# Reordering the planned front of a hybrid encoder layer: S5 output quarters among the attention projections, first scores behind the gated linear unit, row and output-matrix tiles in halves

## The chip, the cores and the metric

One Trainium2 chip, one of its cores, one launch per run. The metric is device time in microseconds (us); a figure quoted as "the time" is the median of three runs.

## The reference

One encoder layer on 1024 tokens of width 1024. The input projection feeds three mixers, whose concatenated outputs go through one output matrix; a mixture of 16 experts follows.

```python
x = layer_norm(x, ln_in_g, ln_in_b)
proj = h @ w_in                    # q,k,v,g of retention | u of S5 | q,k,v of attention
ret  = retention(q, k, v, g, theta)            # 8 chunks of 128 tokens, 4 heads
y    = gelu(S5 states -> outputs + d * u)      # 16 groups of 16 channels
s5   = y * sigmoid(y @ w_glu + b_glu)          # the gated linear unit
att  = window_sink_attention(q, k, v, sink)    # 8 heads, 128-key window, blocks of 128 queries
h    = LN(alpha*h + concat(ret, s5, att) @ w_out)
h    = LN(alpha*h + ExpertChoiceSwiGLU(h))     # 16 experts, width 2048
```

## The kernel before

Every fp32 product of a projection is made of three matmuls on a high and a low half (`mm3`, L74 to L76); `split` writes the high half on ScalarE (ACT, L65 or L125) and the low half on VectorE (DVE, L66).

The work up to the attention scores is `front()`. It is a list of places: `at(place, fn)` gives a step a number, and the steps are then issued in the order of those numbers, so each engine's order is written out by hand. Its parts, in the order of the program:

- The input rows are normed (`Norm`: load `x`, L147 statistics, L152 the power `l0rs` on GpSimd (POOL), L155 and L158 on DVE), turned, and split into the row tiles `hT` (high and low, all 1024 tokens each). Beside that a chain of small operations on POOL (`rsmall`, L254 to L262) works out the retention decays, and ACT takes their exponentials (`w` L266, `dec` L268). The rows of keys and values of chunk 0 follow (`ktok` L193).
- A string `order` then names products: `K`, `V` and `g` (keys, values, gates), `r0` to `r7` (retention outputs), `q00` to `q31` (attention query quarters, 24 matmuls each, whose results go through `kst` and `q_d` stores), and `o0` to `o3`, the S5 output quarters (`Output.product`, L798 and L801, from the tiles `MU`, `W`, `Z`, and `Output.put`, a Gelu on ACT into `YG`, L805). Before, the `o` quarters stand last.
- Behind `o3` the gated linear unit (GLU): four `turn` (transposes of `YG`, L813, then `yT` on ACT, L814), four `gate` (L819) and four `gated` (L827).
- `Matrix` loads the output matrix in four pieces of 1 MB (L901) and splits each into `WO` (ACT L65, DVE L66). `hT` and `WO` take turns in the same two buffers of the pool `hy`: no piece of `WO` can be written until the last product has read `hT`.

Behind `front()` the order on each engine is set by a scheduler that simulates the program. There `attention_keys` loads the keys `KHL` (four 512 KB transfers, L1250) and values `AV` (two, L1252), and `attention_scores(i)` loads `qs` (L1275), all three issued by POOL; it multiplies scores (L1283, L1284), takes the maximum on DVE (L1286) and the exponential on ACT (L1291, L1293). `attention_out(i)` scales (L1307), turns (`pT`, L1313) and multiplies with `AV` (`po`). The output projection multiplies `yh`, `yl` with `WO`. The expert stage is again in a hand-written order and streams 402 MB of weights.

Of the kernel before, what the change touches and what calls it, by code (L numbers as in the profile page):

```python
# [15 lines left out]
OP = mybir.AluOpType  # L16
# [114 lines left out]


class Norm:

# [34 lines left out]
    def parts(self, q):  # L169
        K = self.K  # L170
        ts = slice(self.t * P, (self.t + 1) * P)
        split(K, K.hT[0][:, q * 4:q * 4 + 4, ts], K.hT[1][:, q * 4:q * 4 + 4, ts], self.pt.pop(q))


class Project:
# [5 lines left out]
    def part(self, c0, c1):  # L181
        K, ts = self.K, slice(self.t * P, (self.t + 1) * P)
        if c0 == 0:
            self.ps = K.pmm.tile([P, 512], F32, name="mm")
        for c in range(c0, c1):
            w = self.W[c // 4].u[c // 2 % 2]
            b = [x.rearrange("p (c f) -> p c f", c=2)[:, c % 2, :] for x in w]
            mm3(K.nc, self.ps, [K.hT[s][:, c, ts] for s in range(2)], b, c == 0, c == KC - 1)

# [40 lines left out]
def retention_consts(K, I):  # L230

    nc, cp = K.nc, K.ret
    small = cp.tile([P, 12, 8], F32, name="rsmall")
    th = small[:, 0, :]
    nc.sync.dma_start(th, bcast(I["ret_theta"], 8))
# [11 lines left out]
    nc.scalar.activation(ab, th, AF.Abs)  # L247
    nc.scalar.activation(y, ab, AF.Exp, scale=-1.0)
    po = nc.gpsimd
    ops = [lambda: nc.vector.tensor_scalar(r, y, 2.0, None, op0=OP.add),  # L250
           lambda: nc.vector.reciprocal(r, r),
           lambda: nc.vector.tensor_tensor(s, y, r, OP.mult),
           lambda: nc.vector.tensor_tensor(s2, s, s, OP.mult),
           lambda: po.tensor_scalar(acc, s2, 1.0 / 17, 1.0 / 15, op0=OP.mult, op1=OP.add)]  # L254
    for n in (13, 11, 9, 7, 5, 3, 1):
        ops.append(lambda: po.tensor_tensor(acc, acc, s2, OP.mult))
        ops.append(lambda n=n: po.tensor_scalar(acc, acc, 1.0 / n, None, op0=OP.add))
    ops += [lambda: po.tensor_tensor(acc, acc, s, OP.mult),
            lambda: po.tensor_scalar(mn, th, 0.0, None, op0=OP.min),
            lambda: po.tensor_scalar(acc, acc, -2.0, None, op0=OP.mult),  # L260
            lambda: po.tensor_tensor(lgf, acc, mn, OP.add)]
    ops += [lambda a=a: po.tensor_tensor(K.w2[:, :, a], lg[:, a, :], col[:, a:a + 1].to_broadcast([P, 4]), OP.mult)  # L262
            for a in range(2)]

    def decays():
        nc.scalar.activation(K.w2, K.w2, AF.Exp)  # L266
        for a in range(2):
            nc.scalar.activation(K.dec[a * 64:(a + 1) * 64, :], lg[a * 64:(a + 1) * 64, a, :], AF.Exp, scale=float(P))  # L268
    return ops, decays

# [44 lines left out]
class Turned:  # L315
# [5 lines left out]
    def part(self, c0, c1):  # L321
        K = self.K
        if c0 == 0:
            self.ps = K.pmm.tile([P, 512], F32, name="mm")
        for c in range(c0, c1):
            mm3(K.nc, self.ps, cols([self.units.u[self.m]], c, KC, P, 0, P),
                [K.hT[s][:, c, self.half * 512:(self.half + 1) * 512] for s in range(2)], c == 0, c == KC - 1)

# [5 lines left out]
class Chunk:  # L334
# [9 lines left out]
    def gate_part(self, units, c0, c1):  # L344
        K = self.K
        if c0 == 0:
            self.pg = K.pmm.tile([P, 512], F32, name="mm")
        for c in range(c0, c1):
            mm3(K.nc, self.pg[:, 0:256], [K.hT[s][:, c, self.ts] for s in range(2)], cols(units.u, c, 4, 256, 0, 256),
                c == 0, c == KC - 1)  # L350
# [542 lines left out]
class Matrix:  # L893


    def __init__(self, K, I):
        self.K, self.I, self.raw = K, I, {}

    def load(self, c):
# [3 lines left out]
    def parts(self, c):  # L903
        K = self.K
        if c == 0:
            K.WO = [K.hy.tile([P, KC, D], F32R, name=f"WO{s}", tag="hy") for s in range(2)]
        for i in range(2):
            split(K, K.WO[0][:, c + i, :], K.WO[1][:, c + i, :], self.raw[c][:, i, :])

# [25 lines left out]
def front(K, I, pool, close):  # L935
# [34 lines left out]
    spread(3.5, 0.01, ops[0:4])  # L970
    at(4.0, norm[0].stats)
# [22 lines left out]
    S0, T = 14.0, 7.5  # L994
    at(S0 + 6.5, decays)
    tables, exps = retention_tables(K)
# [3 lines left out]
    for t in range(NT):  # L1000
# [6 lines left out]
        at(s + T + 0.05, p.rows)  # L1007
        at(s + T + 0.6, p.decayed)
        at(s + T + 2.0, p.turn)
        at(s + T + 2.7, p.keys)  # L1010
        at(s + T + 5.3, p.sums)
        at(s + T + 5.8, p.state)
        if t + 1 < NT:
# [196 lines left out]
    at(where["r7"] - 1.0, lambda: router_weights(K))  # L1210
    R = where["r7"] + 2.9 + 12.1
# [13 lines left out]
    at(where["o1"] + 3.1, lambda: out.states(*qs[3], X["s5o"][1]))  # L1225
    G = s + 1.0
    mq = [(m, q) for q in range(2) for m in range(2)]
    for i, k in enumerate(mq):
        at(G + i * 0.6, lambda k=k: out.turn(*k))
        at(G + 2.6 + i * 2.0, lambda k=k: out.gate(*k))  # L1230
        at(G + 4.6 + i * 2.0, lambda k=k: out.gated(*k))
    at(G + 12.0, lambda: (out.store(0), out.store(1)))
    at(G + 12.5, lambda: close(X["s5o"][0], X["s5m"][0]))
# [7 lines left out]
    return X["ast"][0], X["early"][0]  # L1241

# [25 lines left out]
def attention_scores(K, i):  # L1268
# [20 lines left out]
    nc.vector.tensor_scalar(nm, m, -1.0, None, op0=OP.mult)  # L1289
    nc.vector.tensor_tensor(es, K.sink[:, hs], m, OP.subtract)  # L1290
    nc.scalar.activation(es, es, AF.Exp)  # L1291
    for g in range(4):
        nc.scalar.activation(S[g][:, :W], S[g][:, :W], AF.Exp, bias=nm[:, g:g + 1], accum_out=rs[:, g:g + 1])  # L1293
    K.P[i] = S, sm

# [44 lines left out]
def out_proj_part(K, t, n, c0=0, c1=KC):  # L1340
# [6 lines left out]
    for c in range(c0, c1):  # L1347
        mm3(nc, K.ps, (yh[:, c], yl[:, c]), [K.WO[s][:, c, ns] for s in range(2)], c == 0, c == KC - 1)
    if c1 < KC:
# [565 lines left out]
def idle(K, n):  # L1915

    ps = K.pmm.tile([P, 512], F32, name="gu" if K.pmm is K.__dict__.get("pg") else "mm")
    for i in range(n):
        K.nc.tensor.matmul(ps, K.WO[0][:, 0, 0:P], K.WO[0][:, 0, 0:512], start=True, stop=True)

# [182 lines left out]
def build(tc, nc, I, O):  # L2103
# [48 lines left out]
    K.QT = K.ret.tile([P, 2, L], F32, name="QT")  # L2152
    K.hT = [K.hy.tile([P, KC, L], F32R, name=f"hT{s}", tag="hy") for s in range(2)]
    T = mybir.EngineType
    with tc.manual_schedule(engines={T.PE, T.Activation, T.DVE, T.Pool, T.SP}):
        c_ast, c_early = front(K, I, pool, close)
    c_kv, K.kv = pool("kv", side="right")
    attention_keys(K)
    K.mr, K.st, K.pr = {}, {}, {}
    c_at2, K.at2 = pool("at2", side="right")  # L2160
    K.P, K.Y = {}, {}
    ahead = 0
    for _ in range(2):
        attention_scores(K, ahead)
        ahead += 1
    c_op, K.op = pool("op")
# [8 lines left out]
    for i in range(2 * NT + 1):  # L2175
# [3 lines left out]
        if ahead <= i < 2 * NT:  # L2179
            attention_scores(K, i)  # L2180
        t, n = divmod(i - 1, 2)
        if 0 <= t < NT:
# [112 lines left out]
```

## Time and profile before

| | us |
|---|---|
| runs | 1685.55, 1682.06, 1691.47 |
| median | 1685.55 |
| profiled execution, its own time | 1691.02 |
| its span | 1689.3 |
| TensorE (PE) busy in the span | 1613.1 |
| DVE, ACT, POOL busy | 1404.7, 1131.3, 212.8 |

Busy time counts an engine from the start of an instruction to its end; matmuls overlap, so a busy PE isn't a PE at its peak. In the rows below, the number in brackets is the time that an engine was idle just before an instruction, and behind the arrow stands what released it. The granted clock of PE is a share of full speed.

### The profile page before, as it was taken

The numbers are of one execution on the slowest core, as the hardware profiler recorded it, in microseconds if no ns is written. First come the engines' busy times: TensorE is split into PE (matmuls) and PEld (weight loads), VectorE is DVE, ScalarE is ACT, GpSimd is POOL, SyncE is SP. The second block draws the span as 40 slices with busy tenths as digits, with TensorE's granted clock in tenths as the row PEclk, the third lists the DMA queues.
The fourth block names the chain that finished last, engine by engine and source line by source line (L and its number), as shares of the span: only waits on it lengthen the run. The fifth ranks groups of instructions, "written<-read, shape, count | busy, mean of one in ns | idle before, by whom it ended". The sixth has DMA issues, their size and how long they took to land.

```text
span 1689.3 us, 21215 instructions
## 1 busy us (share of the span) xinstructions
PE 1613.1 (95%) x7748; PEld 1299.9 (77%) x7748; DVE 1404.7 (83%) x1712; ACT 1131.3 (67%) x1270; POOL 212.8 (13%) x243
## 2 busy tenths in 40 slices
PE   7999997799998999999999999999999999999997
PEld 5888886587776788888888888888888778777775
DVE  7986863556768998998888989889888999989986
ACT  4644454746654677777777777777777777777773
POOL 3002111000101010101101011010111303131121
PEclk9999998799999999999999999999999999999999
DMA  5466479622315899999999999999999999999993
GB/s 195 175 164 148 121 232 289 185 75 63 101 63 228 317 377 390 409 380 384 363 385 372 381 377 376 389 365 378 387 369 402 401 391 408 380 400 389 379 379 156
DMA packets 105243, 512.04 MB, mean 303 GB/s; under 512 B 13233, under 2 KB 28337, under 8 KB 54450
## 3 DMA queue, kind: packets, MB, share of 16 engines
q1 hardware_dynamic: 88354, 479.75, 74.5%
q0 software_dynamic: 16784, 30.94, 6.6%
q8 instruction: 61, 1.00, 0.2%
q14 instruction: 44, 0.36, 0.1%
HBM read 464.50 MB, written 46.14 MB: 302 GB/s over the span
## 4 chain that ended last, share of the span: by engine, by line
PE 59%; DVE 13%; DMA 11%; issue 8%; ACT 7%; POOL 1%; SPq 1%; DVEq 0%; POOLq 0%; ACTq 0%
PE gu L1772 26%; PE y L1772 13%; DVE whl L1819 6%; PE mm L74 4%; DMA wraw<-in_exp_w_down 4%; PE mm L76 4%; PE mm L75 4%; DMA zz<-acc_d 3%; ACT whl L1812 2%; PE tp L1757 2%; ACT S L1293 1%; DMA wraw<-in_exp_w_up 1%; ACT S L1307 1%; PE tp L1313 1%; DVE zz L2026 1%
## 5 line engine op out<-in xcount | busy, mean ns | idle before, releaser
L1819 DVE TENSOR_TENSOR whl<-wraw,whl 128x2048 fp32r<-128x2048 f32 x384 | 873.3, 2288 | 100.2 <-ACT whl L1812 99.5
L1812 ACT ACTIVATE whl<-wraw 128x2048 fp32r<-128x2048 f32 x384 | 734.8, 1917 | 247.0 <-PE gu L1772 87.7
L1772 PE MATMUL gu<-whl,xT 128*128 128x512 f32 x3072 | 740.9, 397 | 0.0
L1772 PEld LDWEIGHTS gu<-whl,xT 128*128 128x128 f32 x3072 | 570.9, 189 | 125.4
L1772 PE MATMUL y<-whl,hT 128*128 128x512 f32 x1536 | 368.6, 395 | 0.7 <-ACT hT L65 0.7
L1772 PEld LDWEIGHTS y<-whl,hT 128*128 128x128 f32 x1536 | 288.3, 188 | 69.8 <-ACT hT L65 0.9
L1746 POOL DMA_INDIRECT xs<-h_d,index x15 | 41.2, 2749 | 738.9 <-PE y L1772 552.9
L74 PE MATMUL mm<-hT,whl 128*128 128x512 f32 x160 | 65.8, 411 | 1.2 <-DVE kst L883 1.2
L65 ACT ACTIVATE hT<-tp 128x512 fp32r<-128x512 f32 x80 | 46.1, 584 | 30.9 <-PE tp L167 16.4
L76 PE MATMUL mm<-hT,whl 128*128 128x512 f32 x160 | 63.5, 397 | 0.0
L75 PE MATMUL mm<-hT,whl 128*128 128x512 f32 x160 | 63.3, 396 | 0.0
L66 DVE TENSOR_TENSOR hT<-tp,hT 128x512 fp32r<-128x512 f32 x80 | 54.1, 683 | 4.9 <-ACT hT L65 4.8
L74 PE MATMUL mm<-WO,yh 128*128 128x512 f32 x128 | 52.9, 413 | 2.4 <-ACT yh L65 2.2
L1757 PE MATMUL tp<-ident,hid 128*128 128x128 f32 x256 | 39.5, 277 | 16.0 <-DVE hid L1854 16.0
L1757 PEld LDWEIGHTS tp<-ident,hid 128*128 128x128 f32 x256 | 31.3, 142 | 27.9 <-DVE hid L1854 20.6
L75 PE MATMUL mm<-WO,yh 128*128 128x512 f32 x128 | 51.6, 403 | 0.0
L76 PE MATMUL mm<-WO,yl 128*128 128x512 f32 x128 | 50.7, 404 | 0.0
L1286 DVE CUSTOM_DVE_ANT_0 S<-at,R,sink 128x384 f32<-128x384 f32 (+1 forms) x64 | 35.4, 579 | 17.7 <-PE at L1284 15.4
L1293 ACT ACTIVATE S<-S,asm 128x384 f32<-128x384 f32 (+1 forms) x64 | 36.9, 579 | 19.2 <-DVE asm L1289 16.0
L74 PE MATMUL mm<-whl,hT 128*128 128x512 f32 (+1 forms) x128 | 47.7, 373 | 1.6 <-DVE kst L883 1.1
L76 PE MATMUL mm<-whl,hT 128*128 128x512 f32 (+1 forms) x128 | 44.7, 349 | 1.2 <-DVE hT L66 1.2
L1854 DVE TENSOR_TENSOR hid<-hid,gu 128x512 f32<-128x512 f32 x64 | 43.5, 680 | 1.8 <-PE gu L1772 1.8
(433 smaller groups left out, 1824.8 us busy)
## 6 DMA issues: line engine op xcount, KB each, us to landing
wraw<-in_exp_w_gate SPq DMA_DIRECT2D x128, 1024.0 KB, 7.4
wraw<-in_exp_w_up SPq DMA_DIRECT2D x128, 1024.0 KB, 8.5
wraw<-in_exp_w_down SPq DMA_DIRECT2D x128, 1024.0 KB, 7.4
wraw<-in_w_in SPq DMA_DIRECT2D x8, 1024.0 KB, 7.5
x<-in_x SPq DMA_DIRECT2D x8, 512.0 KB, 4.6
h_d<-x SPq DMA_DIRECT2D x8, 512.0 KB, 3.2
q_d<-kst SPq DMA_DIRECT2D x32, 128.0 KB, 3.0
qs<-q_d POOLq DMA_DIRECT2D x16, 256.0 KB, 4.3
```

Of the source, the lines that this page charges most:

```text
L65: nc.scalar.activation(hi, src, AF.Copy)
L66: eng.tensor_tensor(lo, src, hi.bitcast(F32), OP.subtract)
L74: nc.tensor.matmul(ps, a[0], b[0], start=start, stop=False)
L75: nc.tensor.matmul(ps, a[0], b[1], start=False, stop=False)
L76: nc.tensor.matmul(ps, a[1], b[0], start=False, stop=stop)
L1293: nc.scalar.activation(S[g][:, :W], S[g][:, :W], AF.Exp, bias=nm[:, g:g + 1], accum_out=rs[:, g:g + 1])
L1746: nc.gpsimd.indirect_dma_start(out=xs, out_offset=None, in_=K.h1_dram, in_offset=bass.IndirectOffsetOnAxis(ap=K.index[:, e:e + 1], axis=0))
L1757: K.nc.tensor.transpose(pt[:, c, :], src[:, (c0 + c) * P:(c0 + c + 1) * P], K.ident)
L1772: nc.tensor.matmul(ps, a[s][c], u[:, t, i * w:(i + 1) * w], start=first and id(ps) not in began, stop=last and left[id(ps)] == 0)
L1812: self.K.nc.scalar.activation(u[:, 0, :], self.raw[k1].rearrange("p a b -> p (a b)"), AF.Copy)
L1819: self.K.nc.vector.tensor_tensor(u[:, 1, :], raw, u[:, 0, :].bitcast(F32), OP.subtract)
L1854: at(self.after, q, 3, lambda: nc.vector.tensor_tensor(self.h[q], self.h[q], self.pg[q][1], OP.mult))
```

## The change

- The row tiles `hT` and the output matrix `WO` become halves (by tokens, by rows of the matrix); `hy` has four buffers of half the size.
- In `order` the retention outputs from `r2` on move forward by about one product, and the S5 quarters stand among the last attention quarters: `q11 q20 o0 q30 o1 q21 o2 o3 q31`. The GLU follows `q31`.
- `WO` pieces 0 and 2 are written behind `o1` and inside `q21`, pieces 4 and 6 behind `q31`. Their loads move forward.
- `attention_keys` and the first two blocks of scores and exponentials become steps of `front()`: keys and values at `q31`'s end, scores behind the GLU. `attention_scores` is cut in two (`attention_exp` is the new half).
- At the start `x` is the first load; the load of `ret_theta` moves behind the first weight load. The small decay operations are placed behind the first split of `hT`, with the norm's power between them, and their exponentials and chunk 0's keys, sums and state stand a slot later.
- The router's weights move from `r7` to `q20`.

```diff
     rows = Rows(K, I, ln)
-    ops, decays = retention_consts(K, I)
+    ops, decays, theta = retention_consts(K, I)
+    norm[0].load()
     rows.load_shift()
-    norm[0].load()
     rows.load_gain()
     WK[0].load()
+    theta()
...
-    spread(3.5, 0.01, ops[0:4])
...
+    spread(9.95, 0.001, ops[0:5])
...
-    spread(10.3, 0.01, ops[4:])
+    spread(10.3, 0.01, ops[5:14])
...
-    at(S0 + 6.5, decays)
+    spread(S0 + 6.2, 0.01, ops[14:])
+    at(S0 + 8.0, decays)
...
-    order = "K0 g0 g1 K1 r0 V0 r1 g2 g3 V1 r2 q00 r3 g4 g5 q10 r4 q01 r5 g6 g7 r6 q11 r7 q20 q30 q21 q31 o0 o1 o2 o3".split()
+    order = "K0 g0 g1 K1 r0 V0 r1 g2 r2 g3 V1 r3 q00 g4 r4 g5 q10 r5 g6 r6 q01 g7 r7 q11 q20 o0 q30 o1 q21 o2 o3 q31".split()
...
-    G = s + 1.0
+    G = s + 0.3
...
-    X["mat"] = Matrix(K, I)
-    at(where["q31"] + 5.7, lambda: close(K.c_hl))
-    for i in range(4):
-        at(where["q20"] + 1 + i if i < 2 else where[f"o{i - 1}"] + 0.5, lambda i=i: X["mat"].load(2 * i))
-        at(where[f"o{i}"] + 3.3, lambda i=i: X["mat"].parts(2 * i))
+    mat = Matrix(K, I)
+    at(where["q01"], lambda: mat.load(0))
+    at(where["q11"] + 8.2, lambda: mat.load(2))
+    at(where["o1"] + 0.3, lambda: (mat.parts(0), mat.load(4)))
+    at(where["q21"] + 3.0, lambda: (mat.parts(2), mat.load(6)))
+    at(where["q31"] + 6.0, lambda: mat.parts(4))
+    at(G + 3.0, lambda: mat.parts(6))
+    def keys():
+        close(K.c_hl)
+        X["kv"] = pool("kv", side="right")
+        K.kv = X["kv"][1]
+        attention_keys(K)
+        X["at2"] = pool("at2", side="right")
+        K.at2 = X["at2"][1]
+    at(where["q31"] + 5.7, keys)
+    for i in range(2):
+        at(G + 10.3 + i * 2.6, lambda i=i: attention_scores(K, i))
+        at(G + 12.9 + i * 2.6, lambda i=i: attention_exp(K, i))
...
-    c_hy, K.hy = pool("hy", bufs=2)
+    c_hy, K.hy = pool("hy", bufs=4)
```

**ACT, from the first output quarter on.** Before, these rows stand together (YG is the Gelu of an output quarter, S and asm the exponentials of a score block, WO a split of the output matrix):

```order
L805 ACT_TABLE_LOAD
L805 ACTIVATE YG<-mm 128x4x8x16
L65 ACTIVATE WO_2973<-wraw 128x1024 x2
L805 ACTIVATE YG<-mm 128x4x8x16
L65 ACTIVATE WO_2973<-wraw 128x1024 x2
L1293 ACT_TABLE_LOAD
L1293 ACTIVATE S,asm<-S,asm 128x256
L1291 ACTIVATE asm<-asm 128x4
L1293 ACTIVATE S,asm<-S,asm 128x256 x3
L1307 ACTIVATE S<-S,asm 128x256 x4
```

Of the change, the same engine up to the first exponential (kst is the result of an attention quarter; the Gelu table is loaded three rows ahead of these):

```order
L65 ACTIVATE WO_2905<-wraw 128x1024 x2
L814 ACTIVATE YG<-mm 128x4x8x16
L65 ACTIVATE WO_2905<-wraw 128x1024 x2
L851 ACTIVATE kst<-mm,qscale 128x512
L814 ACTIVATE YG<-mm 128x4x8x16 x2
L851 ACTIVATE kst<-mm,qscale 128x512
L823 ACTIVATE yT<-tp 128x512
L65 ACTIVATE WO_3038<-wraw 128x1024 x2
L823 ACTIVATE yT<-tp 128x512 x3
L65 ACTIVATE WO_3038<-wraw 128x1024 x2
L836 ACTIVATE glu<-mm,hb 128x512 x4
L1331 ACT_TABLE_LOAD
```

The Gelus moved in among the results of the attention quarters, no exponential stands between two of them any more, and the tables are loaded once for all four Gelus and once for the exponentials.

**POOL, the transfers for the attention.** Before, three query loads stand ahead of keys and values:

```order
L1275 DMA qs<-q_d_0_75 128x4x128
L399 TENSOR_TENSOR rrs<-rve,mhalf 128x4 x2
L1275 DMA qs<-q_d_1_76 128x4x128
L1275 DMA qs<-q_d_0_75 128x4x128
L1250 DMA KHL_3089<-k_d_103 128x2x512
L1250 DMA KHL_3089<-k_d_105 128x2x512
L1250 DMA KHL_3090<-k_d_104 128x2x512
L1250 DMA KHL_3090<-k_d_106 128x2x512
L1252 DMA AV<-v_d_107 128x2x512
L1252 DMA AV<-v_d_108 128x2x512
```

With the change:

```order
L408 TENSOR_TENSOR rrs<-rve,mhalf 128x4
L1281 DMA KHL_3019<-k_d_103 128x2x512
L1281 DMA KHL_3019<-k_d_105 128x2x512
L1281 DMA KHL_3020<-k_d_104 128x2x512
L1281 DMA KHL_3020<-k_d_106 128x2x512
L1283 DMA AV<-v_d_107 128x2x512
L1283 DMA AV<-v_d_108 128x2x512
L1306 DMA qs<-q_d_0_75 128x4x128
L1306 DMA qs<-q_d_1_76 128x4x128
```

All query loads moved behind keys and values.

**ACT, at the start.** Before, from the first split of `hT` to the keys of chunk 0:

```order
L65 ACTIVATE hT_166<-tp 128x4x128 x2
L266 ACTIVATE w_187<-w_187 128x8
L268 ACTIVATE dec<-lg 64x4 x2
L477 ACTIVATE sm<-sm 128x16
L193 ACTIVATE ktok<-mm 128x256
L195 ACTIVATE kv<-mm 128x256
L201 ACTIVATE k_381<-ktok,w_187 128x64 x8
```

With the change:

```order
L65 ACTIVATE hT_166<-tp 128x4x128 x2
L486 ACTIVATE sm<-sm 128x16
L200 ACTIVATE ktok<-mm 128x256
L202 ACTIVATE kv<-mm 128x256
L275 ACTIVATE w_188<-w_188 128x8
L277 ACTIVATE dec<-lg 64x4 x2
L506 ACTIVATE sm<-sm 128x16
```

The decays' exponentials `w` and `dec` moved from in front of `ktok` to behind it.

## Rows read from the trace of the kernel before

**Rows 1.** Windows by stage: start:end, length, busy PE, PEld, DVE, ACT, POOL, clock, DMA share, GB/s.

```profile
50.00:250.00 200.00, 194.12 (x1158) 164.19 (x1158) 157.05 (x403) 102.27 (x230) 21.39 (x37) 0.99 0.58 163
250.00:350.00 100.00, 82.41 (x376) 62.59 (x375) 45.58 (x115) 58.92 (x124) 10.87 (x20) 0.86 0.71 219
600.00:1600.00 1000.00, 989.63 (x4532) 800.28 (x4530) 904.71 (x598) 752.85 (x547) 124.72 (x70) 1.00 0.99 385
```

**Rows 2.** Timeline of PE from 262 to 352 us: start, length, engine, line, operation.

```profile
264.67 0.50 PE L74 MATMUL mm<-hT,whl 128*128 128x512 f32 x1 [1.19 <-DVE kst L883]
...
270.28 0.38 PE L798 MATMUL mm<-MU 128*128 128x128 f32 x2
...
272.96 0.39 PE L798 MATMUL mm<-MU 128*128 128x128 f32 x2
...
280.81 0.55 PE L1283 MATMUL at<-KHL,qs 128*128 128x256 f32 x1 [4.79 <-DMA KHL<-k_d]
...
304.97 1.12 PE L813 MATMUL tp<-ident,YG 128*128 128x128 f32 x4 [4.66 <-ACT YG L805]
...
309.11 5.66 PE L819 MATMUL mm<-yT,wg 128*128 128x512 f32 x8
...
315.48 3.60 PE L819 MATMUL mm<-yT,wg 128*128 128x512 f32 x8
...
350.60 0.41 PE L76 MATMUL mm<-WO,yl 128*128 128x512 f32 x1
```

**Rows 3.** Windows of a few microseconds, columns as in the first group.

```profile
29.00:33.00 4.00, 3.94 (x13) 3.04 (x14) 3.12 (x10) 2.67 (x12) 0.56 (x1) 0.62 0.19 70
280.00:285.00 5.00, 4.19 (x19) 4.20 (x20) 3.39 (x8) 0.65 (x1) 0.74 (x1) 0.50 1.16 382
```

**Rows 4.** Timeline of ACT around the first Gelu and the last retention turn.

```profile
258.02 0.69 ACT L842 ACTIVATE kst<-mm,qscale 128x512 fp32r<-128x512 f32 x1 [5.04 <-PE mm L76]
258.61 0.37 ACT L421 ACTIVATE roT<-tp 128x256 f32<-128x256 f32 x1
...
273.19 1.28 ACT L805 ACT_TABLE_LOAD   x1 [2.02 <-PE mm L801]
274.49 0.60 ACT L805 ACTIVATE YG<-mm 128x512 f32<-128x512 f32 x1
```

**Rows 5.** Timeline of all engines from 27.9 to 29.1 us.

```profile
27.98 0.21 ACT L266 ACTIVATE w<-w 128x8 f32<-128x8 f32 x1 [5.78 <-POOL w L262]
...
28.50 1.28 DVE L158 SCALAR_TENSOR_TENSOR x<-x,l0rs,bb 128x1024 f32<-128x1024 f32 x1 [2.08 <-POOL l0rs L152]
...
29.07 0.33 PE L207 MATMUL tp<-ident,ktok 128*128 128x128 f32 x1 [1.84 <-ACT ktok L193]
```

**Rows 6.** Timeline of SP's queue: start and length of DMA issues.

```profile
259.01 0.33 SPq L422 DMA_DIRECT2D y_d<-roT  x1
260.85 0.34 SPq L766 DMA_DIRECT2D wg<-in_ssm_w_glu  x1
...
263.60 0.90 SPq L790 DMA_DIRECT2D Z<-s_d  x2
```

**Rows 7.** DMA, 270 to 300 us: packets, MB, share; issues with KB each, us to landing.

```profile
q0 software_dynamic: 4272, 4.46, 59.3%
q1 hardware_dynamic: 2087, 5.30, 51.1%
...
KHL<-k_d POOLq DMA_DIRECT2D x4, 512.0 KB, 10.4
...
Z<-s_d SPq DMA_DIRECT2D x4, 256.0 KB, 7.6
AV<-v_d POOLq DMA_DIRECT2D x2, 512.0 KB, 21.0
```

**Rows 8.** Timeline of POOL: issue of the four key transfers.

```profile
273.25 2.79 POOL L1250 DMA_DIRECT2D KHL<-k_d  x4
```

**Rows 9.** The key tile's matmuls by line: count, shortest, median, longest in ns.

```profile
L1283 PE MATMUL at<-KHL,qs x26: 279/417/626, 280.8 to 331.2; 128*128 128x384 f32 x18, 128*128 128x256 f32 x8
```

More of the change, by code (lines that the diff above doesn't have):

```diff
@@ L130, in low, with token_slice @@
         self.K.nc.vector.tensor_tensor(lo, self.raw[:, i, :], hi.bitcast(F32), OP.subtract)
+def token_slice(t):
+    half, i = divmod(t, NT // 2)
+    return half, slice(i * P, (i + 1) * P)
 class Norm:
@@ L170, in parts @@
         K = self.K
-        ts = slice(self.t * P, (self.t + 1) * P)
-        split(K, K.hT[0][:, q * 4:q * 4 + 4, ts], K.hT[1][:, q * 4:q * 4 + 4, ts], self.pt.pop(q))
+        half, ts = token_slice(self.t)
+        hi, lo = (K.hT[s][half][:, q * 4:q * 4 + 4, ts] for s in range(2))
+        split(K, hi, lo, self.pt.pop(q))
 class Project:
@@ L181, in part @@
     def part(self, c0, c1):
-        K, ts = self.K, slice(self.t * P, (self.t + 1) * P)
+        K, (half, ts) = self.K, token_slice(self.t)
         if c0 == 0:
@@ L187, in part @@
             b = [x.rearrange("p (c f) -> p c f", c=2)[:, c % 2, :] for x in w]
-            mm3(K.nc, self.ps, [K.hT[s][:, c, ts] for s in range(2)], b, c == 0, c == KC - 1)
+            mm3(K.nc, self.ps, [K.hT[s][half][:, c, ts] for s in range(2)], b, c == 0, c == KC - 1)
     def rows(self):
@@ L268, in decays @@
             nc.scalar.activation(K.dec[a * 64:(a + 1) * 64, :], lg[a * 64:(a + 1) * 64, a, :], AF.Exp, scale=float(P))
-    return ops, decays
+    return ops, decays, lambda: nc.sync.dma_start(th, bcast(I["ret_theta"], 8))
 def retention_tables(K):
@@ L326, in part @@
             mm3(K.nc, self.ps, cols([self.units.u[self.m]], c, KC, P, 0, P),
-                [K.hT[s][:, c, self.half * 512:(self.half + 1) * 512] for s in range(2)], c == 0, c == KC - 1)
+                [K.hT[s][self.half][:, c, :] for s in range(2)], c == 0, c == KC - 1)
 def query_rows(K, p, m, half):
@@ L344, in gate_part @@
     def gate_part(self, units, c0, c1):
-        K = self.K
+        K, (half, ts) = self.K, token_slice(self.t)
         if c0 == 0:
@@ L348, in gate_part @@
         for c in range(c0, c1):
-            mm3(K.nc, self.pg[:, 0:256], [K.hT[s][:, c, self.ts] for s in range(2)], cols(units.u, c, 4, 256, 0, 256),
+            mm3(K.nc, self.pg[:, 0:256], [K.hT[s][half][:, c, ts] for s in range(2)], cols(units.u, c, 4, 256, 0, 256),
                 c == 0, c == KC - 1)
@@ L897, in __init__ @@
         self.K, self.I, self.raw = K, I, {}
+        K.WO = [], []
     def load(self, c):
@@ L904, in parts @@
         K = self.K
-        if c == 0:
-            K.WO = [K.hy.tile([P, KC, D], F32R, name=f"WO{s}", tag="hy") for s in range(2)]
+        if c % 4 == 0:
+            for s in range(2):
+                K.WO[s].append(K.hy.tile([P, KC // 2, D], F32R, name=f"WO{s}", tag="hy"))
         for i in range(2):
-            split(K, K.WO[0][:, c + i, :], K.WO[1][:, c + i, :], self.raw[c][:, i, :])
+            hi, lo = (K.WO[s][c // 4][:, c % 4 + i, :] for s in range(2))
+            split(K, hi, lo, self.raw[c][:, i, :])
 class Rows:
@@ L1007, in front @@
         at(s + T + 0.05, p.rows)
[L1008 to L1012, printed above, removed]
+        late = 0 if t else T
+        at(s + late + T + 0.6 - late / 20, p.decayed)
+        at(s + late + T + 2.0 - late / 20, p.turn)
+        at(s + late + T + 2.7 - late / 20, p.keys)
+        at(s + late + T + 5.3 - late / 4, p.sums)
+        at(s + late + T + 5.8 - late / 4, p.state)
         if t + 1 < NT:
@@ L1209, in front @@
             at(where[prev[i]] + 8.0, lambda wt=wt, i=i: wt.low(i))
-    at(where["r7"] - 1.0, lambda: router_weights(K))
+    at(where["q20"], lambda: router_weights(K))
     R = where["r7"] + 2.9 + 12.1
@@ L1290, in attention_scores, with attention_exp @@
     nc.vector.tensor_tensor(es, K.sink[:, hs], m, OP.subtract)
+    K.P[i] = S, sm
+def attention_exp(K, i):
+    nc = K.nc
+    c = i // 2
+    W = (min(c + 2, NT) - max(c - 1, 0)) * P
+    S, sm = K.P[i]
+    m, nm, rs, es, rd = (sm[:, k] for k in range(5))
     nc.scalar.activation(es, es, AF.Exp)
@@ L1347, in out_proj_part @@
     for c in range(c0, c1):
-        mm3(nc, K.ps, (yh[:, c], yl[:, c]), [K.WO[s][:, c, ns] for s in range(2)], c == 0, c == KC - 1)
+        mm3(nc, K.ps, (yh[:, c], yl[:, c]), [K.WO[s][c // 4][:, c % 4, ns] for s in range(2)], c == 0, c == KC - 1)
     if c1 < KC:
@@ L2152, in build @@
     K.QT = K.ret.tile([P, 2, L], F32, name="QT")
-    K.hT = [K.hy.tile([P, KC, L], F32R, name=f"hT{s}", tag="hy") for s in range(2)]
+    K.hT = [], []
+    for half in range(2):
+        for s in range(2):
+            K.hT[s].append(K.hy.tile([P, KC, L // 2], F32R, name=f"hT{s}", tag="hy"))
+    K.P, K.Y = {}, {}
     T = mybir.EngineType
     with tc.manual_schedule(engines={T.PE, T.Activation, T.DVE, T.Pool, T.SP}):
-        c_ast, c_early = front(K, I, pool, close)
-    c_kv, K.kv = pool("kv", side="right")
-    attention_keys(K)
+        c_ast, c_early, c_kv, c_at2 = front(K, I, pool, close)
     K.mr, K.st, K.pr = {}, {}, {}
[L2160 to L2165, printed above, removed]
+    ahead = 2
     c_op, K.op = pool("op")
```

25 lines of the change are left out of this document (13 added, 12 removed).

## The prediction

> **What bounds the kernel now.** I read the windows by stage first. From 600 us on PE is busy 989.6 of 1000 us at the full clock, and the DMA engines 0.99 of the time [rows 1]; nothing in the change touches that stage, and a stage that works without gaps passes on whatever time it is started earlier. The gaps lie ahead of it: from 50 to 250 us PE is busy 194 of 200 us, from 250 to 350 us only 82.4 of 100, at a granted clock of 0.86 [rows 1]. That is 17.6 us of idle time, and some of the rest at the lower of the clock's two levels (1.2 GHz instead of 2.4): the clock is 0.50 from 280 to 285 us [rows 3]. This is where the change works.
>
> The PE timeline there shows who was waited for [rows 2]. The last attention quarter q31 runs from 264.67 to 270.28 us, 5.6 us; an S5 output quarter takes 2.68 us (270.28 to 272.96). Two quarters later PE waits 4.79 us for the keys, which POOL can only issue once `hl` is free, at 273.25 us [rows 8]. Before the GLU it waits 4.66 us for `YG` of ACT at 304.97 us, because Gelus and exponentials alternate on ACT and the scheduler put the last Gelu behind two score blocks. Each alternation is a table load of 1.28 us [rows 4], of which ACT's timeline holds six from 273 to 322 us. The GLU's first eight records take 5.66 us on the low clock, the last eight 3.60 us; it ends at 319.08. The first output-projection tile is complete at 351.0.
>
> **The start.** PE waits 1.84 us for `ktok`, which stands on ACT behind `w`, which waits for the POOL chain of decays; DVE waits 2.08 us for `l0rs`, last in that chain [rows 5]. Right behind the wait the clock falls to 0.62 for 4 us [rows 3], which costs 4 x 0.38 = 1.5 us of full-speed work. Both waits have no cause left when `w` stands behind `ktok` and `l0rs` inside the chain. Against it: four small DVE operations and two of ACT now stand beside the first split of `hT`, an estimated 0.5 us at the 0.2 us of ACT's `w`. Sum 1.84 + 1.5 - 0.5 = 2.8 us; bounds 1.3 (the clock falls anyway) and 3.3 (the small operations cost nothing). The pulled-forward `r` items fill no gap that I could price: the 6 us of idle time from 50 to 250 us [rows 1] are many small ones, so they are costed at nothing.
>
> **Front's tail, until q31 ends.** The quarters up to q20 are done at 252.3 before: 264.67 less the 1.19 us that DVE's `kst` held q31 and two quarters of 5.6. With 2.8 us gained this is E = 249.5. What is left for PE is three quarters and four S5 quarters, 3 x 5.6 + 4 x 2.68 = 27.5 us. New waits come in. A product can only start in a PSUM tile that an earlier result has left, and q30 waits for the Gelu of o0. That Gelu needs the S5 space, which opens when the last retention store `y_d` has landed: on SP the next issue stands 1.84 us behind it (259.01 to 260.85) [rows 6]. From E: `kst` 0.69 and the last retention turn 0.37, store 1.84, table 1.28, Gelu 0.60 [rows 4, 6], together 4.8, while o0 ends at E + 2.7: a wait of 2.3 us (a row of this dependency doesn't exist; bounds 0 and 4). Then o1 waits for its states `Z`: issued some 4.6 us behind the store on SP [rows 6], landing after 7.6 us in the median [rows 7], against o1's earliest start behind q30: 1.8 us (0 to 4). o3's `Z` the same, 1.0. The low clock behind these waits costs about 1.4. q31 ends at T = E + 27.5 + 2.3 + 1.8 + 1.0 + 1.4 = 283.5 us. DVE and ACT have room for the splits of `WO` (45.6 and 58.9 of 100 us busy [rows 1]); they are costed at nothing while they lie under q21 and the GLU's transposes. If they were late, the GLU's gates would wait, 1 us at most.
>
> **GLU.** Between the first `turn` and the first gate 4.1 us pass (304.97 to 309.11), the gates take 2 x 3.60 at the full clock, and about 1 us goes to waits for `kst` of q31 and for the PSUM tile: the end is at T + 12.3 = 295.8, where before it was 319.08. By this milestone the change has gained 23 us.
>
> **What it gives back.** Before, keys, values and queries travelled while the S5 quarters and the GLU ran, and three score blocks were done before the GLU. Now the keys are issued at T, and the first queries stand behind keys and values on POOL (order rows above). POOL's four issues of keys take 2.79 us [rows 8], two more for the values half of that, so the queries are issued at T + 4.2. The software queue moved 4.46 MB at a share of 59.3% of 30 us [rows 7], 17.8 us; keys (2.10 MB), values (1.05) and one query tile (0.26) are 3.41 MB, or 13.6 us alone. Two expert weight loads of 1 MB are released by the same `WO` splits and travel beside them: 2.1 MB at the hardware queue's pace (5.30 MB in 51.1% of 30 us, 15.3 us) is 6.1 us. Low bound for the landing of the first queries: T + 13.6, no collision; high bound: T + 25, since before the values landed 21.0 us after their issue, which is 2.79 us behind the first key's: 23.8 us [rows 7, 8]. I take T + 19.5, all of the collision, since before both queues together had filled the engines too. PE then stands idle for some 7 us behind the GLU, and the first scores run at the low clock.
>
> The Trainium skill, "DMA: Bandwidth & Descriptors", section "Anatomy of one DMA", gives a GpSimd-issued transfer about 2 us and its bytes at 436 GB/s. By that the 3.41 MB would be there 9.8 us after the issue, so before the GLU ends, and nothing would be given back. The row above stands against it: two issues of 512 KB landed after 21 us.
>
> From the queries' landing on PE repeats what it did from 319.08 to 351.0 us, 31.9 us, and also the three score blocks it had done before: 12 score pairs, some 0.40 us each beyond the overlap of the two matmuls (a single one takes 0.417 in the median [rows 9]), 4.8 us. The first output-projection tile is complete at T + 19.5 + 36.7 = 339.7 against 351.0. Gain 11.3 us, which the attention and the experts behind it pass on.
>
> **Sum.** Against the profiled execution's own time 1691.02 - 11.3 = 1679.7; that execution is 5.5 us above the median of the three runs, so for the median 1685.55 - 11.3 = 1674.3 us. I say 1674.
>
> **Rivals.**
> - *Keys arrive in time* (landing at T + 13.6, or the waits in the tail don't appear): 5.9 us more, gain 17 to 20, about 1667 us. For it: the queue alone is fast enough. Against it: the 21 us of the values [rows 7]. Chance 0.2.
> - *The waits eat most of it*: queries at T + 24, or each wait in the tail at its upper bound (another 4 us), and a clock that stays low through the idle stretch. Gain 3 to 8, about 1680 us. For it: the low clock behind each of the long waits [rows 3]. Chance 0.23.
> - *The software queue makes it slower*: with the landing at T + 30.8 (351.0 - 36.7 - 283.5) the gain is nought. If the queue needs what it needed before (23.8 us to the last value), plus the query tile (0.26 MB, 1 us), plus the two weight loads (6.1), it is T + 31, and PE, idle for 18 us, works on the low clock for some 10 us, which costs 5 us more: 1691 us. It needs both queues at their slowest together. To be slower by more than 0.5% the landing must be later than T + 39, or the scheduler's changed order of the attention has to lose time as well. Chance 0.11.
> - *Nothing arrives at the end*: the attention from 350 us on has its own pace, because the scheduler's order there is different too, and the gain in front of it melts to within 2 us, 1685 us. Against it: PE's work there is unchanged. Chance 0.06.
>
> **Numbers.** The forecast itself, 1670 to 1678 us, has 0.4. Its bounds come from the start (1.3 to 3.3), the tail's waits and the landing. The range for 8 in 10 runs from 1664, the first rival at its best, to 1687, which leaves out the slow half of the third. 0.5% of the median is 8.4 us, about what a measurement of this kernel tells from no change. Faster by more than that: the first rival whole, the forecast's 0.4 but for its slow fifth of 0.05, and a small part (0.05) of the second: 0.6. Slower by more than that: 0.07, most of the third rival. The rest, 0.33, is within.
>
> **What the changed profile would show.** The wait for `ktok` at 29 us is gone, and the clock doesn't fall behind it. There is one Gelu table load and one exponential load between 245 and 320 us, instead of six. PE waits about 2 us for `YG` of ACT ahead of q30. The GLU ends 20 to 24 us earlier. Behind it PE waits 5 to 9 us for a query or key transfer, at a low clock; the first output-projection tile is complete near 340 us. From 600 us on the stages are the same length. I am wrong if the GLU's end moves by less than 15 us (the tail's waits were mis-sized), if there is no wait behind the GLU (the queue was), or if the tile at 340 us is right and the end isn't earlier by as much (the attention's own order).

## The result, and the profile after

The changed kernel takes 1677.56 us in the median of 20 runs, the kernel before 1691.45 us in the median of 20: a ratio of 0.992 (95% interval 0.9902 to 0.9938), 13.9 us less. The forecast was 1674 us, 11.3 us less than the 1685.55 of three runs, with a range of 1664 to 1687. Those three lay 5.9 us below the median of all 20, so the two gains are the better pair to compare. The profiled execution of the change took 1681.89 us.

The number came out; the places didn't. The windows of the changed kernel, columns as in [rows 1]:

```profile
29.00:33.00 4.00, 4.00 (x22) 3.07 (x21) 2.65 (x11) 1.47 (x6) 2.47 (x11) 1.00 0.75 258
250.00:350.00 100.00, 74.43 (x341) 57.56 (x340) 41.58 (x100) 47.59 (x104) 11.02 (x20) 0.85 0.71 214
```

The low clock behind 29 us is gone (0.62 in [rows 3]). It didn't come with the wait for `ktok` each time, though. In a second profile of the kernel before (e_before, below) that wait is there, 1.89 us, and the clock in the same window is 1.00:

```profile
29.00:33.00 4.00, 3.65 (x23) 3.19 (x24) 3.41 (x10) 3.09 (x14) 0.56 (x1) 1.00 0.10 37
```

The stage that the change rebuilds is emptier than before: PE is busy 74.4 of 100 us, where it was 82.4 [rows 1]. Its timeline says why, as [rows 2] did before:

```profile
257.70 0.79 PE L74 MATMUL mm<-hT,whl 128*128 128x512 f32 x1 [5.89 <-ACT YG L814]
...
279.67 0.49 PE L810 MATMUL mm<-W,Z 128*128 128x128 f32 x2 [2.59 <-DMA Z<-s_d]
...
281.42 0.79 PE L810 MATMUL mm<-W,Z 128*128 128x128 f32 x2 [1.25 <-DMA Z<-s_d]
...
295.27 8.62 PE L828 MATMUL mm<-yT,wg 128*128 128x512 f32 x16
...
314.88 0.55 PE L1314 MATMUL at<-KHL,qs 128*128 128x256 f32 x1 [10.98 <-DMA qs<-q_d]
```

q30 waits 5.89 us for the first Gelu, o3 3.84 us for its states, and behind the GLU, which ends at 303.9 us (15.2 us earlier than before, where 20 to 24 were forecast), PE waits 10.98 us for the first query tile. SP's queue shows what the Gelu waited for (start and length of the issues):

```profile
249.80 0.53 SPq L911 DMA_DIRECT2D wraw<-in_w_out  x1
250.43 0.39 SPq L431 DMA_DIRECT2D y_d<-roT  x1
255.66 0.33 SPq L775 DMA_DIRECT2D wg<-in_ssm_w_glu  x1
```

The issue behind the last retention store stands 5.2 us behind it, 1.84 us in [rows 6]; a 1 MB load of the output matrix (`wraw`) was issued just ahead of the store. ACT's timeline has one Gelu table load and one for the exponentials, as the order of the program said:

```profile
255.75 1.28 ACT L814 ACT_TABLE_LOAD   x1 [5.63 <-DMA y_d<-roT]
...
304.63 1.28 ACT L1331 ACT_TABLE_LOAD   x1
```

POOL issued keys, values and queries one behind the other:

```profile
291.34 2.94 POOL L1281 DMA_DIRECT2D KHL<-k_d  x4 [52.67 <-PE mm L76]
294.27 1.42 POOL L1283 DMA_DIRECT2D AV<-v_d  x2
295.69 2.23 POOL L1306 DMA_DIRECT2D qs<-q_d  x3
```

The first scores, which wait for the first query tile, thus start 24.0 us after q31's end at 290.9.

So the front gained little. Before, the 48th matmul of the output projection, which starts at 350.60 us, ended its first tile [rows 2]. In the change the 48th stands 2.3 us earlier, where 11.3 were forecast:

```profile
348.32 0.48 PE L76 MATMUL mm<-WO,yl 128*128 128x512 f32 x1
```

By the work done even that is gone. SP's queue has a row that marks the attention's pace, the store of a finished tile of 128 tokens (`acc_d`); the first and the last one of the kernel before, and then of the changed one:

```profile
373.42 0.32 SPq L1453 DMA_DIRECT2D acc_d<-ah  x1
...
529.41 0.32 SPq L1453 DMA_DIRECT2D acc_d<-ah  x1
```

```profile
378.08 0.86 SPq L1492 DMA_DIRECT2D acc_d<-ah  x1
...
523.30 0.32 SPq L1492 DMA_DIRECT2D acc_d<-ah  x1
```

The first tile is finished 4.7 us later than before, the last one 6.1 us earlier. The windows, columns as in [rows 1], from the first tile's store to PE's first turn (transpose) of the expert candidates (`cand`, my mark for the attention's end), before and after:

```profile
373.42:519.09 145.67, 136.13 (x719) 105.85 (x717) 100.13 (x278) 84.94 (x205) 15.91 (x47) 0.96 0.26 83
```

```profile
378.08:512.98 134.90, 129.57 (x709) 102.66 (x708) 97.06 (x270) 84.53 (x204) 14.62 (x45) 0.99 0.27 88
```

145.7 us became 134.9. PE's idle time in it went from 9.5 to 5.3 us, the mean clock from 0.96 to 0.99 (some 4 us), and ten instructions of PE fewer were left to do. Counted from the same work, the last 719 matmuls of PE ahead of `cand`, the attention starts 3.0 us later than before (375.8 us against 372.8) and takes 137.1 us instead of 146.3. None of the attention's own code was changed in substance. What changed is the order in which the scheduler put it. The kernel before has two long waits of PE in this stretch, both for ACT. The first is for `rows`:

```profile
410.60 0.66 PE L1313 MATMUL tp<-ident,S 128*128 128x128 f32 x4 [2.82 <-ACT rows L1561]
```

In the second, ACT copies a result `yh` behind four exponentials that wait for DVE, and PE waits for `yh`:

```profile
435.72 0.62 ACT L1293 ACTIVATE S<-S,asm 128x384 f32<-128x384 f32 x1 [2.21 <-DVE asm L1289]
...
438.13 0.19 ACT L1293 ACTIVATION_READ_ACCUMULATOR S<-S,asm 128x1 f32 x1
438.35 0.59 ACT L65 ACTIVATE yh<-po 64x512 fp32r<-64x512 f32 x1
```

```profile
438.99 0.50 PE L74 MATMUL mm<-WO,yh 128*128 128x512 f32 x1 [2.24 <-ACT yh L65]
```

In the changed kernel `yh` stands ahead of the exponentials, and PE waits for neither of the two:

```profile
436.77 0.59 ACT L65 ACTIVATE yh<-po 64x512 fp32r<-64x512 f32 x1
...
439.06 0.62 ACT L1333 ACTIVATE S<-S,asm 128x384 f32<-128x384 f32 x1 [1.08 <-DVE asm L1320]
```

### The profile page after: what moved, and what is told of

The parts are those of the page before. It is cut to its first block, busy times and chain, and to the rows that moved or that the text cites. A ratio compares the mean times of both kernels' runs of the same rounds, so it can differ in the third digit from the quotient of the medians.

```text
span 1680.2 us, 21213 instructions
## 1 busy us (share of the span) xinstructions
PE 1603.5 (95%) x7748; PEld 1296.0 (77%) x7748; DVE 1402.9 (84%) x1712; ACT 1126.6 (67%) x1266; POOL 212.7 (13%) x243
## 4 chain that ended last, share of the span: by engine, by line
PE 59%; DVE 13%; DMA 11%; issue 9%; ACT 6%; POOL 1%; SPq 0%; POOLq 0%; DVEq 0%; ACTq 0%
PE gu L1811 25%; PE y L1811 13%; DVE whl L1858 6%; PE mm L74 4%; DMA zz<-acc_d 4%; PE mm L76 4%; PE mm L75 4%; DMA wraw<-in_exp_w_down 3%; ACT whl L1851 2%; PE tp L1796 2%; DMA wraw<-in_exp_w_gate 1%; DMA qs<-q_d 1%; PE tp L1352 1%; DMA wraw<-in_exp_w_up 1%; PE sm L1455 1%
## 5 line engine op out<-in xcount | busy, mean ns | idle before, releaser
L74 PE MATMUL mm<-whl,hT 128*128 128x512 f32 (+1 forms) x128 | 47.3, 370 | 0.1
L76 PE MATMUL mm<-whl,hT 128*128 128x512 f32 (+1 forms) x128 | 44.7, 349 | 1.2 <-DVE hT L66 1.2
L75 PE MATMUL mm<-whl,hT 128*128 128x512 f32 (+1 forms) x128 | 45.1, 352 | 0.5 <-DVE whl L130 0.5
## 6 DMA issues: line engine op xcount, KB each, us to landing
x<-in_x SPq DMA_DIRECT2D x8, 512.0 KB, 4.6
h_d<-x SPq DMA_DIRECT2D x8, 512.0 KB, 3.2
```

The lines of the kernel that those rows point to most:

```text
L74: nc.tensor.matmul(ps, a[0], b[0], start=start, stop=False)
L75: nc.tensor.matmul(ps, a[0], b[1], start=False, stop=False)
L76: nc.tensor.matmul(ps, a[1], b[0], start=False, stop=stop)
```

## The experiments

My theory after these rows: the front lost what it gained to three waits of its own making (the store behind the load, the states, the queries behind keys and values), and the attention's new order made the gain. The rival is the one that I had forecast: the front's gain reaches the end, and the attention has a pace of its own that hides some of it.

### e_store: the output matrix's load behind the last retention store

```diff
-    at(where["q11"] + 8.2, lambda: mat.load(2))
+    at(O + 0.03, lambda: mat.load(2))
```

> The change, with one step moved: the load of output-matrix piece 2 (1 MB) is issued behind the last retention store and the S5 loads instead of just ahead of that store. Theory: the 5.9 us that PE waits for the first Gelu ahead of q30 is the store's landing behind the 1 MB transfer on the same queue (5.2 us there, 1.84 us before). Then the store lands in about 2 us, the wait falls to 2 to 3 us, q31 ends about 3 us earlier, at 287 to 288 us, and the end follows by 2 to 4 us. Rival: the wait is ACT's or SP's own queue; then it stays above 5 us and nothing moves.

Measured: 1685.08 us, 0.9963 (0.995 to 0.9977) of the kernel before, 7.5 us slower than the change. The wait behaved as expected: the next issue stands 1.94 us behind the store, and q30 waits 2.33 us.

```profile
249.55 0.33 SPq L431 DMA_DIRECT2D y_d<-roT  x1
251.49 0.34 SPq L775 DMA_DIRECT2D wg<-in_ssm_w_glu  x1
```

```profile
253.54 0.79 PE L74 MATMUL mm<-hT,whl 128*128 128x512 f32 x1 [2.33 <-ACT YG L814]
```

The first tile was stored at 370.1 us, 8 us earlier than in the change. But the attention ended at 512.0, 1 us earlier. 7 us were lost on the way, and PE waits for `yh` again, 2.24 us near 430 us. So the cause of the wait ahead of q30 is shown, but the end didn't follow, and neither the theory nor its rival had expected that.

### e_query: the first queries ahead of the keys

```diff
+    for i in range(2):
+        at(where["q31"] + 0.5, lambda i=i: attention_queries(K, i))
     at(where["q31"] + 5.7, keys)
```

(`attention_queries` is the load taken out of `attention_scores`.)

> The change, with the first two query tiles loaded ahead of the keys on POOL instead of behind keys and values. Theory: the 11 us that PE waits behind the GLU are the queries' place in POOL's queue; with it undone the wait is 0 to 2 us (the first key tile landed 4 to 8 us after its issue at q31's end, the GLU takes 13), the scores start at the clock that the GLU leaves, and the attention ends 9 to 12 us earlier, the whole kernel 8 to 12 us. Rival: the keys and values themselves are late, or the attention runs at its own pace; then PE waits for keys or values instead, and less than 4 us reach the end.

Measured: 1670.81 us, 0.9881 (0.9863 to 0.9899). The first scores start at 296.71 us, as soon as the GLU leaves PE, without a wait; the next wait is for DVE, 2.65 us.

```profile
277.31 1.49 POOL L1304 DMA_DIRECT2D qs<-q_d  x2 [38.07 <-DMA Z<-s_d]
286.41 2.79 POOL L1283 DMA_DIRECT2D KHL<-k_d  x4 [7.61 <-PE mm L76]
```

```profile
296.71 0.69 PE L1323 MATMUL at<-KHL,qs 128*128 128x256 f32 x1
```

First tile at 364.8, attention's end at 499.5: 13.3 and 13.5 us ahead of the change. Here the whole gain passes to the attention's end. The 11 us were the queries' place in POOL's queue. The median is 6.8 us below the change's, less than the 8 to 12 expected; the profiled execution is the slowest of the five and lies 5.3 us above the median.

### e_all: both, and the states of o3 ahead of a quarter's stores

```diff
-    at(where["o1"] + 3.1, lambda: out.states(*qs[3], X["s5o"][1]))
+    at(where["o1"] + 1.7, lambda: out.states(*qs[3], X["s5o"][1]))
```

> Both of these, and the states Z of the last S5 quarter issued ahead of an attention quarter's stores instead of behind them. Theory: the three waits are independent and add: q31 ends 5 to 7 us earlier than in the change, and the whole kernel is 13 to 18 us faster than the change. Rival: they share one cause, the load on the DMA engines, and the sum is no more than the larger of the two.

Measured: 1672.52 us, 0.9902 (0.9883 to 0.9922), no better than the queries alone. In the front most of the gains add: the first tile comes at 360.2 us, 17.9 us ahead of the change, where e_store alone had 7.9 and e_query 13.3. The attention's end is 2.0 us behind e_query's, at 501.5, with the wait for `yh` back:

```profile
422.00 0.50 PE L74 MATMUL mm<-WO,yh 128*128 128x512 f32 x1 [2.23 <-ACT yh L65]
```

So the theory's end didn't come. The time is what the rival said, no better than the larger of the two gains, but not for its reason: in the front the gains are there, and they are lost behind it.

### e_start: the kernel before, with the start edits alone

```diff
+    norm[0].load()
     rows.load_shift()
-    norm[0].load()
...
-    spread(10.3, 0.01, ops[4:])
+    spread(10.3, 0.01, ops[5:14])
```

(and the other edits of the start, as in the change)

> The kernel before, with the start edits alone (x as the first load, theta behind the first weights, the norm's power inside the decay chain, the decays and chunk 0's products a slot later). Theory: the waits for ktok (1.84 us) and for the power (2.08 us) and the low clock behind them go, q20 ends 2.5 to 3 us earlier, and the end too, 1.3 to 3.3 us. Rival: chunk 0's products only move the wait, and the end doesn't move by more than 0.5 us.

Measured: 1687.21 us, 0.9976 (0.996 to 0.9992). The waits for `ktok` and the power are gone. In the front little is left of them: q31 starts at 263.47 us, against 264.67 in the first profile of before and 263.14 in its second. New waits stand in their place: the first turns of `x` start 0.9 us later in the change than before, and a turn waits 0.7 us for ACT's `kv` at 39 us. Of the 4 us, 2.7 come in the attention (143.0 us from first tile to end, instead of 145.7). Its order is 0.98 like that of before, but of the two waits of before only that for `rows` (2.83 us) is there, and that for `yh` isn't.

### e_all2: the load two places earlier on SP, and with it another order of the attention

```diff
-    at(where["q11"] + 8.2, lambda: mat.load(2))
+    at(O + 0.015, lambda: mat.load(2))
```

(with the other two edits of e_all)

> The queries ahead of the keys, the Z of the last S5 quarter ahead of the stores, and output-matrix piece 2 behind the last retention store as in the run with all three, but two places earlier on SP, ahead of the Z of o1. By the listing of the programs the attention's order on PE is then word for word that of the run with the queries alone, where the run with all three had another. Theory, that the attention's order decides what reaches the end: the first tile's rows are stored 2 to 4 us earlier than with the queries alone (364.8 us), and all of it passes: the attention ends at 496 to 498 us (499.5 with the queries alone, 501.5 with all three). Rival, that the attention has a pace of its own which takes back what the front gains: it ends at 499 to 502 us again.

Measured: 1670.33 us, 0.9866 (0.9841 to 0.9891). The front was not faster: the load now stands ahead of o1's states, and PE waits at the first product that reads them. The profile names no releaser here, so that it is the states is an inference.

```profile
263.45 1.42 PE L810 MATMUL mm<-W,Z 128*128 128x128 f32 x4 [3.38 <-issue]
```

First tile at 365.4, end at 499.5, the same as e_query, with the same order. That fits the theory, but since the front's gain failed to come it doesn't tell it from the rival.

### e_nostart: the change without its start edits

```diff
-    at(S0 + 8.0, decays)
+    at(S0 + 6.5, decays)
```

(and the rest of the start as before)

> The change without its edits at the start. Their worth in the front is 1 to 2.8 us. But by the listing the attention's order on PE is then another one, 0.91 like that of the run with all three and 0.82 like the change's. Theory, that this order costs some 6 us as it did in the runs e_store and e_all: the first tile's rows are stored 1 to 3 us later than in the change (378.1), the attention ends 5 to 10 us later (513.0 in the change), so at or near the 519.1 of before, and the median is 5 to 10 us above the change. Rival, that the change's gain doesn't hang on this order: both are 1 to 3 us later.

Measured: 1685.35 us, 0.9964 (0.9947 to 0.9982), 7.8 us above the change (5.6 above e_again, the change run once more), as the theory said. The rest of the expectation missed: the first tile came at 373.8 us, earlier than in the change and not later, and the attention took 141.0 us and ended at 514.8. That is 1.9 us later than in the change's first profile, where 5 to 10 were expected, and 6.0 later than in its second. The edits at the start gave the front nothing here: without them o0 starts at 248.66 us, with them at 248.97 and 249.26.

### e_sched: the first scores handed back to the scheduler

```diff
-    for i in range(2):
-        at(G + 10.3 + i * 2.6, lambda i=i: attention_scores(K, i))
-        at(G + 12.9 + i * 2.6, lambda i=i: attention_exp(K, i))
...
+    for i in range(2):
+        attention_scores(K, i)
+        attention_exp(K, i)
```

> The change, with the first two score blocks handed back to the scheduler; keys and values stay in the front. The query loads still stand behind keys and values. Theory, that the queries' landing decides when the scores start: PE waits for a query behind the GLU again, 8 to 11 us, and the scores start at 313 to 316 us. What the end does hangs on the attention's order, which is a third one (0.69 like the change's): anything from 0 to +8 us against the change. Rival, that the place of the scores in the front made the wait: it shrinks below 5 us.

Measured: 1683.05 us, 0.9938 (0.9913 to 0.9963). The expectation of 8 to 11 us rested on a misreading, and the wait shrank as the rival said: the scheduler put the query loads ahead of the keys on POOL by itself, and PE waits for a key tile only:

```profile
291.87 0.36 PE L1311 MATMUL at<-KHL,qs 128*128 128x256 f32 x1 [2.54 <-DMA KHL<-k_d]
```

First tile at 366.6 us, 11.5 us ahead of the change; then 141.7 us for the attention, which ends at 508.2. It says the same of the queries as e_query, and the same of the order as e_all. The seven times fall into two groups, 1674 to 1676 and 1683 to 1685 us, and the profiled execution is one of the lower, so its attention's end can't be set beside the median.

### e_order: all three moves, and the router's weights one product later

```diff
-    at(where["q20"], lambda: router_weights(K))
+    at(where["q21"], lambda: router_weights(K))
```

(with all of e_all)

> The run with all three moves, and the router's weights one product later (q21 instead of q20). Nothing else in the front changes, but by the listing the attention's order on PE is now word for word that of the run with the queries alone. Theory, that this order decides how much of the front's gain reaches the end: the first tile's rows are stored at 359 to 362 us as with all three (360.2), and the attention ends at 494 to 497 us instead of 501.5; the wait of 2.23 us for yh near 422 us is gone; the median is 4 to 7 us below that run's 1672.5. Rival, that the attention takes back by its own pace what the front gains: 499 to 502 us, median unchanged.

Measured: 1664.15 us, 0.9845 (0.9819 to 0.9871). First tile at 361.0 us, within 1 us of e_all; the attention ends at 495.15, 6.3 us earlier than there. The two windows, e_all's and then e_order's:

```profile
360.22:501.49 141.27, 132.67 (x711) 103.81 (x710) 98.39 (x271) 84.35 (x204) 14.71 (x46) 0.98 0.26 85
```

```profile
361.02:495.15 134.13, 129.60 (x711) 102.27 (x710) 97.05 (x271) 84.52 (x204) 14.73 (x46) 0.99 0.27 89
```

The same 711 instructions of PE, 7.1 us less. Idle time falls from 8.6 to 4.5 us. The medians differ by 8.4 us. In the traces PE's order over its last 719 matmuls ahead of `cand` is the same in e_order, e_query and e_all2, instruction for instruction, and another in e_all. Here the work is the same, the fronts end within 1 us of each other, and the order differs: the order is the cause, and the rival, a pace that the attention keeps whatever its order, is out.

### e_flip, e_again and e_before: the change with the router's weights moved, and both kernels again

```diff
-    at(where["q20"], lambda: router_weights(K))
+    at(where["o0"], lambda: router_weights(K))
```

> The change, with nothing but the router's weights moved by half a product (behind q20 instead of at it). By the listing the attention's order on PE becomes that of the slower kind (0.94 like that of e_store, 0.83 like the change's). Theory: the front is as in the change, within a microsecond or two, but the attention ends 4 to 8 us later against its first tile, a wait for yh of 2.24 us shows near the third tile, and the median is 4 to 8 us above the change, at about 1683. Rival, that the order doesn't matter: the median stays within 2 us of the change.

> The change once more, for a second profile. In the first one o3 waited 3.8 us for its states, in the runs e_nostart and e_sched about 1.1 us with the same front there, and that execution lies 4.3 us above the median. If this is only the landing of one transfer, the second profile has q31 end at 286 to 288 us instead of 291, the first tile stored near 374 and the attention's end near 508; if the change's front makes that wait, it repeats within 0.5 us.

> The kernel before once more, for a second profile: how far its stages move from one execution to the next. The attention ended at 519.1 us in the first; the same to within 2 us is expected, with waits of 2.8 us for rows near 410 us and 2.24 us for yh near 439 us at the same places in the order.

Measured: e_flip 1683.95 us, 0.9957 (0.9939 to 0.9974); e_again 1679.8 us, 0.9931 (0.9909 to 0.9953); e_before one run, 1690.57 us. The windows of e_flip and of e_again:

```profile
369.70:510.77 141.07, 132.91 (x708) 104.36 (x707) 97.50 (x270) 84.41 (x204) 14.61 (x45) 0.96 0.26 84
```

```profile
375.54:508.85 133.31, 127.96 (x709) 101.73 (x708) 96.81 (x270) 84.51 (x204) 14.63 (x45) 1.00 0.27 89
```

Half a product's move of one small step makes the attention 7.8 us longer, and the kernel some 4 us slower than the change run beside it. I had expected the front to stay in place, and it didn't: the first tile came 5.8 us earlier than in e_again, so that the attention's end differs by 1.9 us only. Part of that is the moved step itself: its 16 matmuls, 1.87 us, now run while PE waits for the Gelu anyway. And the wait that I had named, for `yh`, isn't there; in this order PE waits 1.75 us for `rt` and 0.95 us for `pT` instead, on a clock of 0.66 from 450 to 460 us. The class of the order was told by the listing; the wait was not.

The second profile of the change has the wait for o3's states at 1.4 us in place of 3.8, and q31 ends at 288.1; the waits for the Gelu (6.03 us) and for the queries (12.86 us) repeat. So the 3.8 us are one landing's chance (it is 0.9 to 1.1 us in e_query, e_nostart, e_sched and e_flip); the other two waits belong to the change. In the second profile of before the attention's end is 2.3 us earlier, just outside the 2 us expected, with both waits in place (2.83 us for `rows`, 2.24 us for `yh`), and its attention takes 145.6 us again.

All runs beside each other (us; the order's class is that of its likeness to e_query's or e_all's listing):

| run | first tile stored | attention's end | between | median |
|---|---|---|---|---|
| before / e_before | 373.4 / 371.2 | 519.1 / 516.8 | 145.7 / 145.6 | 1691.5 |
| e_start | 371.8 | 514.8 | 143.0 | 1687.2 |
| change / e_again | 378.1 / 375.5 | 513.0 / 508.9 | 134.9 / 133.3 | 1677.6 / 1679.8 |
| e_query, e_all2, e_order (order as the change's) | 364.8, 365.4, 361.0 | 499.5, 499.5, 495.2 | 134.7, 134.2, 134.1 | 1670.8, 1670.3, 1664.2 |
| e_store, e_all, e_nostart, e_flip (the other order) | 370.1, 360.2, 373.8, 369.7 | 512.0, 501.5, 514.8, 510.8 | 141.9, 141.3, 141.0, 141.1 | 1685.1, 1672.5, 1685.4, 1684.0 |
| e_sched (a third) | 366.6 | 508.2 | 141.7 | 1683.1 |

Whatever the front did, the column between has 133 to 135 us with the change's order, 141 to 142 with the others and 146 before; only e_start stands apart at 143. The waits of PE agree with it. In their last 719 matmuls the orders like the change's have no wait above 0.8 us. Each of the others has one or two: 2.2 us for `yh` in e_store and e_all, 1.7 for `rt` and 1.0 for `pT` in e_nostart and e_flip, twice 1.9 to 2.0 for `pT` in e_sched, 2.8 for `rows` in e_start, and 2.8 for `rows` and 2.2 for `yh` before.

## Why the prediction was right, and where it was not

The time lay within the range, and the sum of 11.3 us was near the 13.9 measured. It was near by luck: the step "which the attention and the experts behind it pass on" failed, and so did the sum of the front, and the two errors nearly cancelled.

- **Start.** 2.8 us forecast. The two waits went, but the later turns and a new wait for `kv` gave most of it back: e_start shows about 1.2 us against one profile of before and none against the other. The 1.5 us of low clock in that sum were one execution's: e_before and e_nostart have the wait for `ktok` at 1.9 us and a clock of 1.00 behind it.
- **Up to q20.** E was 249.5 forecast, and o0 starts at 248.97. That isn't the start's doing, since o0 starts at 248.66 in e_nostart. What went are waits that I had costed at nothing. From 230 to 250 us PE has no idle time in the change, where before it was busy 18.7 us, with waits of 0.93 us for the retention output `ro` and 0.35 us for the router's sum `rsum`, and a clock of 0.83 in the second half. Both steps were moved, and no run moves either alone.
- **The wait ahead of q30.** Mis-sized: 2.3 us forecast, 5.9 and 6.0 measured, beyond my upper bound of 4. I took the store's landing from a row where no load lay just ahead of it in the queue, and the change moves a 1 MB load right there. e_store shows that cause. (By its own parts the forecast is 2.1, as 4.8 less 2.7.)
- **The waits for states.** o1's 1.8 us didn't come, o3's was 3.8 and 1.4 us where I had 1.0. The 1.4 us for the low clock behind these waits had no row in the sum. q31 ended at 290.9 and 288.1 us instead of 283.5, and the GLU at 303.9 instead of 295.8 in the first profile, nearly all of it q31's delay.
- **The queries.** The mechanism was right, the size at its upper bound: T + 24.0 instead of T + 19.5, so that PE waited 11 to 13 us and not 7. e_query shows that it was the place in the queue. Before, POOL issued two query tiles at 271.72 us, ahead of the keys; they waited for a store of `q_d`, and so it was this, with q31 over at 270.28, that held the keys until 273.25 and not `hl`. The 21.0 us of the values is the landing of one of the two, the second, issued 3.47 us behind the first key. An estimate by the Trainium skill's formula for a GpSimd-issued transfer (page "DMA: Bandwidth & Descriptors", section "Anatomy of one DMA"), which I had set aside, would have had the 3.41 MB there in 9.8 us; the query tiles issued behind 3 MB in that queue landed after 19.0 us here.
- **The sum of the front.** 11.3 us earlier forecast at the first output-projection tile. By the 48th matmul it was 2.3 us, and the first tile was stored 4.4 to 4.7 us later. Ten more instructions of PE were done by then, some 2 us.
- **The attention.** I costed the scheduler's order at nothing, and priced it only as a loss of the fourth rival. It was worth 11 to 12 us, some 2 of them work done earlier. e_order and e_all, with the same front and the same instructions, differ by 7.1 us through the order alone. The rest, from 141 or 142 us to 146, is the difference between two other orders, and no run isolates it.

What stays open: by the profiles the attention of the change ends 6 to 8 us earlier than before, and the medians differ by 12 to 14. Part of the rest may be the stretch behind the attention, whose code no run changes. From `cand` to the end it took 1165 to 1177 us in these profiles, and 1167.2 and 1174.1 us in the two of the change alone, so a single profile can't place a few microseconds at the end. Nor is it settled how much of the 11 us each wait costs with the low clock behind it.

The fastest version here is e_order, 1664.15 us: the change with the queries ahead of the keys, the load behind the store, the states ahead of the stores, and the router's weights a product later.

## What to carry to other kernels

Where a scheduler orders a later stage from a simulation, an edit ahead of it can redraw that order, as five of the eight variants of the change did here: mark the stage's start and end in the profile, and judge an edit by both, before you credit it with the time at the end. A step that moves a large transfer must be priced by what then stands behind it in its queue, not by the landing of that small transfer when the queue was free. And a small load that a whole stage waits for belongs ahead of the large ones on a queue that works in order.

## What the runs showed of the hardware that was not expected

A 128 KB store that is issued behind a 1 MB load on the same queue held the next issue 5.2 us, where it held it 1.84 to 1.94 us with no such load just ahead. A query tile of 256 KB behind 3 MB on the software queue took 19.0 us to land; with the queries ahead of them (e_query) the median was 5.9 us for a query tile and 7.0 us for a key tile of 512 KB.
